# Causal masks of two attention kinds taken off TensorE, and whole-row running products, in a one-layer hybrid decoder on one Trainium2 core

## The chip, the core and the metric

The kernel runs on one core of a Trainium2 chip. A core has five engines that run their own queues of instructions in order and wait for each other by semaphores: TensorE (PE, with its weight loads shown apart as PEld), VectorE (DVE), ScalarE (ACT), GpSimd (POOL) and SyncE (SP, which here only issues DMAs). The metric is the device time of one execution in microseconds (us); lower is better. Work is in on-chip memory (SBUF, 128 partitions) and in the accumulators of TensorE (PSUM, eight banks).

## The reference

One decoder layer over one sequence of 2048 tokens of width 1024, in float32. The parts that matter here are the two causal attentions, eight heads of width 64 each:

```python
def forgetting_attention(q, k, v, log_f):            # FoX
    F = jnp.cumsum(log_f, axis=-1)
    ...
        s = jnp.einsum('bhqd,bhkd->bhqk', q_blk, k) * scale
        s = s + F_blk[..., None] - F[:, :, None, :]
        causal = kpos[None, :] <= qpos[:, None]
        s = jnp.where(causal, s, -jnp.inf)
        p = jax.nn.softmax(s, axis=-1)

def stick_breaking_attention(q, k, v):
    """A[t,s] = sigmoid(z_ts) * prod_{s<j<t} (1 - sigmoid(z_tj)), s < t"""
    ...
        strict = kpos[None, :] < qpos[:, None]
        log_one_minus_beta = jnp.where(strict, jax.nn.log_sigmoid(-z), 0.0)
        rest = lax.cumsum(log_one_minus_beta, axis=3, reverse=True) - log_one_minus_beta
        a = jnp.where(strict, jnp.exp(jax.nn.log_sigmoid(z) + rest), 0.0)

def reference(x, c, ...):
    h = rms_norm(x, g_attn) * (1.0 + scale_a) + shift_a          # scale, shift, gate from silu(c) @ w_ada
    q_f, k_f, v_f, q_s, k_s, v_s, f_logit = split(h @ w_in)
    log_f = jax.nn.log_sigmoid(f_logit + b_fgate)
    mix = concat(head_rms_norm(fox(...)), head_rms_norm(stick_breaking(...)))
    x = x + gate_a * (mix @ w_out)
    h = rms_norm(x, g_mlp) * (1.0 + scale_m) + shift_m
    u_gate, u_val = split(causal_depthwise_conv(h @ w_up))
    x = x + gate_m * ((silu(u_gate) * u_val) @ w_down)
    return rms_norm(x, g_final)
```

## The kernel before

The kernel works through three stages. First, attention in 32 units: a unit is a kind (`sb` for stick-breaking, then `fox`), a pair of heads `p` (0 to 3) and a block of 512 queries `tb` (0 to 3). While unit i attends, the projections of unit i+1 are interleaved (`interleave`); then follow the output projection, and the gated MLP (up, convolution, down). A scheduler places each instruction on its engine's queue by a simulation of the times, so the order on a queue isn't the order of the code, and projections may run some units ahead. What limits how far is the number of buffers that a tile's tag has: the buffers of a tag are used in turn in the order of the code, and a new tile waits until the last reader of the buffer is done.

Products in float32 precision are made from a high and a low part (`split`: ScalarE rounds the high part, another engine subtracts, lines 43 to 45).

Within a unit, each of two 256-query halves (`j`) and each of the two heads (`hl`) is a call of `sb_head` or `fox_head`. A half has two rows of 128 queries (`qi`). Row `qi` sees `(2 * j + qi + 1) * 128` keys, taken in chunks `ch` of 512 keys. `logits` (lines 382 to 388) makes one chunk in a bank of PSUM from two matmuls (there are two such banks); in the last chunk, which holds the diagonal, a third matmul in bf16 adds 1e30 to the masked places of the last 128 columns. The sign is turned, so that a large logit means no weight.

`sb_head` goes from the last chunk to the first. ScalarE makes `r` = sigmoid and `a` = sigmoid of the negated logits; VectorE turns `r` into a running product from right to left (line 426); `a` is multiplied by it (line 427), on VectorE where `(ch + qi) % 4 == 0` and on GpSimd otherwise. The product so far goes from one chunk's tile into the next as one copied column (line 424, GpSimd). `weighted` (lines 390 to 406) then transposes blocks of `a` on TensorE, splits them (ScalarE line 400, VectorE line 401) and multiplies them with V.

`fox_head` goes from the first chunk to the last. VectorE adds the forget sums `Fb` (a row of the cumulated sums on all partitions, a tile for each block of 512 keys and head) to the logits and keeps the running minimum (line 451), ScalarE takes the exponential of the whole row (line 455), and `weighted` follows.

`forget_sums` (lines 235 to 254) is called once, ahead of unit (sb,1,0). It loads the gate's logits, takes the logarithm of the sigmoid on ScalarE (Abs, Exp, Ln) and VectorE, stores it, loads it back with one head to a partition, and cumulates it in four scans of 512, each from the last column of the one before. Its tiles come from the tags `hf_a` and `z` of pool `px`, which else serve the projections of the first head pair.

`load_w` loads and splits the projection weights of a head pair; for `sb` the low parts are made by VectorE, for `fox` by GpSimd.

Pools lie on a stack: `px` and above it `sx` (tiles of the attention), which are both closed ahead of the first FoX unit, where `fx` is opened. A pool that is opened where others lay waits tile by tile for their last readers.

Of the kernel before, what the change touches and what calls it, by code (L numbers as in the profile page):

```python
# [16 lines left out]
P = 128  # L17
# [16 lines left out]
def kernel(ctx: ExitStack, tc: tile.TileContext, x, c, w_ada, b_ada, g_attn, w_in, b_fgate,  # L34
# [30 lines left out]
    ident = const.tile([P, P], F32, name="ident")  # L65
    make_identity(nc, ident)
    identb = const.tile([P, P], BF16, name="identb")
    make_identity(nc, identb)
    ones = const.tile([P, P], F32, name="ones")
    nc.vector.memset(ones, 1.0)  # L70
    masks = {}
    for kind, base in (("sb", -1), ("fox", 0)):
        m = masks[kind] = const.tile([P, P], BF16, name=f"mask_{kind}")
        nc.vector.memset(m, 0.0)
        nc.gpsimd.affine_select(out=m, in_=m, pattern=[[-1, P]], base=base, channel_multiplier=1,
                                compare_op=ALU.is_ge, fill=BIG)
# [8 lines left out]
    cols = const.tile([P, P + 40], F32, name="cols")  # L85
# [149 lines left out]
    def forget_sums():  # L235
        z = px.tile([NTB * NH, TB], F32, name="fz", tag="hf_a", bufs=2)
        e = px.tile([NTB * NH, TB], F32, name="fe", tag="z", bufs=2)
# [9 lines left out]
        for t in range(NTB):  # L247
            e = px.tile([NH, TB], F32, name="fl", tag="z", bufs=2)
            z = px.tile([NH, TB], F32, name="fc", tag="hf_a", bufs=2)
            nc.sync.dma_start(e, log_f[t * NH:(t + 1) * NH])  # L250
            nc.vector.tensor_tensor_scan(z, e, e, carry, ALU.add, ALU.bypass)
            carry = px.tile([NH, 1], F32, name="carry", bufs=2)
            nc.vector.tensor_copy(carry, z[:, TB - 1:TB])
            nc.sync.dma_start(fs[:, t * TB:(t + 1) * TB], z)

    def load_w(kind, p):
        base = (0 if kind == "fox" else 3 * 512) + p * P
        lo_engine = nc.vector if kind == "sb" else None
# [123 lines left out]
    def logits(kind, cw, need, qcols, hl, Q, K, last):  # L382
        b = qk()
        nc.tensor.matmul(b[:, :cw], Q[:, hl, 0, qcols], K[:, hl, :cw], start=True, stop=False)  # L384
        nc.tensor.matmul(b[:, :cw], Q[:, hl, 1, qcols], K[:, hl, :cw], start=False, stop=not last)  # L385
        if last:
            nc.tensor.matmul(b[:, need - P:need], identb, masks[kind], start=False, stop=True)
# [20 lines left out]
    def sb_head(j, qc, hl, Q, K, V, o):  # L408
        n = (2 * j + 2 + 3) // 4
        right = [None, None]  # L410
        for ch in range(n - 1, -1, -1):
            at = []
            for qi in range(2):
                need = min(512, (2 * j + qi + 1) * P - ch * 512)
                b = logits("sb", max(need, 2 * P), need, slice((qc + qi) * P, (qc + qi + 1) * P), hl, Q, K[ch],
                           ch == n - 1)
                r = sx.tile([P, 512 + 1], F32, name="r", bufs=7)
                a = sx.tile([P, 512], F32, name="a", bufs=7)
                nc.scalar.activation(r[:, :need], b[:, :need], AF.Sigmoid)  # L419
                nc.scalar.activation(a[:, :need], b[:, :need], AF.Sigmoid, scale=-1.0)  # L420
                if right[qi] is None:
                    nc.gpsimd.memset(r[:, need:need + 1], 1.0)
                else:
                    nc.gpsimd.tensor_copy(r[:, need:need + 1], right[qi][:, 0:1])
                rev = r[:, 0:need + 1][:, ::-1]
                nc.vector.tensor_tensor_scan(rev, rev, rev, 1.0, ALU.mult, ALU.bypass)  # L426
                (nc.vector if (ch + qi) % 4 == 0 else nc.gpsimd).tensor_mul(a[:, :need], a[:, :need], r[:, 1:need + 1])  # L427
# [4 lines left out]
            for m in range(0, nk, 2):  # L432
                kts = [4 * ch + m, 4 * ch + m + 1]
                weighted(o, kts, lambda kt, qi: at[qi][:, (kt - 4 * ch) * P:(kt - 4 * ch + 1) * P], V, hl,
                         ch == n - 1 and m == 0, ch == 0 and m == nk - 2, kts[0] == 2 * j)
                yield

    def fox_head(j, qc, hl, Q, K, V, o, Fb, ls):
        n = (2 * j + 2 + 3) // 4
        rows_ = []  # L440
        for qi in range(2):
            W = (2 * j + qi + 1) * P
            a = sx.tile([P, S], F32, name="p", bufs=4)
            mn = None
            for ch in range(n):
                need = min(512, W - ch * 512)
                b = logits("fox", max(need, 2 * P), need, slice((qc + qi) * P, (qc + qi + 1) * P), hl, Q, K[ch],
                           ch == n - 1)
                sl = slice(ch * 512, ch * 512 + need)
                m2 = sx.tile([P, 1], F32, name="mn", bufs=8)  # L450
# [211 lines left out]
    for i, u in enumerate(units):  # L662
        kind, p, tb = u
        nxt = units[i + 1] if i + 1 < len(units) else None
        if u == ("sb", 1, 0):
            forget_sums()
# [357 lines left out]
```

## Time and profile before

| what | us |
|---|---|
| median of 3 runs | 3146.88 |
| the three runs | 3148.08, 3141.64, 3146.88 |
| the profiled execution | 3145.07 |
| its span, first to last instruction | 3143.3 |
| TensorE, busy in the span | 2990.1 (95%) |
| VectorE | 2158.8 (69%) |
| ScalarE | 1652.0 (53%) |
| GpSimd | 1215.3 (39%) |

A row of a group names the line, the engine and the operation, what it writes and reads, the shapes and the count; then the busy time in us, the mean of one in ns, and the engine's idle time just before it with what ended it. A row of a timeline begins with the start in us and the length. A row of the waits gives the time in us, how often, and the longest. Busy time of TensorE includes the modelled ends of pipelined matmuls, so a busy TensorE can still be stalled for part of it. Of 3143.3 us, the stick-breaking units take up to 922 us, the FoX units those up to 1606 us, and the rest of the layer what is left.

### The profile page before, as it was taken

What the parts mean: (1) busy time and instruction counts of PE and PEld (TensorE: products, weight loads), DVE (VectorE), ACT (ScalarE), POOL (GpSimd) and SP (SyncE); (2) the same over time, 40 slices, a digit from 0 to 9 for tenths busy, and PEclk for the clock granted to TensorE, in tenths of its full rate; (3) what the DMA queues carried; (4) which work ended last, traced back from release to release, by engine and by line L of the source; (5) the groups of instructions that cost most, each with busy time, mean ns of one, the idle gap of its engine ahead of it and who ended that gap; (6) DMA issues with size and microseconds to landing.
All of it is one profiled execution on the core that took longest, in us unless ns stands there. A gap on an engine that the chain in (4) does not pass through costs nothing.

```text
span 3143.3 us, 46642 instructions
## 1 busy us (share of the span) xinstructions
PE 2990.1 (95%) x16190; PEld 2521.1 (80%) x16190; DVE 2158.8 (69%) x3343; ACT 1652.0 (53%) x3033; POOL 1215.3 (39%) x1391
## 2 busy tenths in 40 slices
PE   6899998999989999999999999999899998999998
PEld 5778787877878889888877678888678887888887
DVE  6787888978866775556843587777987776254253
ACT  5565666656756665556744444444444444343332
POOL 2563555647543132142112344444444442322321
PEclk8999999999999999999999999999999999999999
DMA  9447542455336695685546632222222223554552
GB/s 267 167 156 247 169 128 78 159 200 161 127 107 225 204 306 184 188 298 177 170 154 219 213 101 81 86 87 82 84 80 83 88 86 123 195 199 161 190 199 90
DMA packets 292941, 496.53 MB, mean 158 GB/s; under 512 B 29449, under 2 KB 177665, under 8 KB 291681
## 3 DMA queue, kind: packets, MB, share of 16 engines
q1 hardware_dynamic: 281072, 480.92, 47.9%
q10 hardware_dynamic: 11632, 12.63, 1.1%
q8 instruction: 128, 2.10, 0.3%
q14 instruction: 109, 0.88, 0.1%
HBM read 352.61 MB, written 90.51 MB: 141 GB/s over the span
## 4 chain that ended last, share of the span: by engine, by line
PE 57%; DVE 13%; DMA 12%; POOL 7%; issue 6%; ACT 4%; SPq 1%; ACTq 0%; POOLq 0%; DVEq 0%
PE ps_pj L287 8%; PE ps_o L963 8%; PE ps_pv L405 6%; PE ps_o L813 6%; PE ps_pt L396 5%; PE ps_pj L326 5%; PE ps_t L963 4%; PE ps_bc L963 4%; DMA wuraw<-in_w_up_dram 3%; PE ps_qk L384 3%; PE ps_qk L385 3%; DVE r L426 2%; DVE wu L45 2%; PE ps_t L813 2%; DMA Q<-q 2%
## 5 line engine op out<-in xcount | busy, mean ns | idle before, releaser
L813 PE MATMUL ps_o<-oa,wu 128*128 128x512 f32 x2088 | 503.3, 392 | 12.6 <-DVE oa L45 7.5
L813 PEld LDWEIGHTS ps_o<-oa,wu 128*128 128x128 f32 x2088 | 390.7, 188 | 104.2 <-DVE oa L45 11.8
L405 PE MATMUL ps_pv<-at,V 128*128 128x256 f32 x2304 | 416.4, 299 | 25.6 <-DVE at L401 12.5
L401 DVE TENSOR_TENSOR at<-ps_pt,at 128x512 fp32r<-128x512 f32 (+1 forms) x576 | 363.4, 651 | 109.1 <-ACT at L400 106.5
L400 ACT ACTIVATE at<-ps_pt 128x512 fp32r<-128x512 f32 (+1 forms) x576 | 315.7, 577 | 209.6 <-PE ps_pt L396 165.8
L287 PE MATMUL ps_pj<-hp,w_qk 128*128 128x512 f32 x1512 | 414.1, 405 | 11.9 <-POOL hp L45 3.4
L426 DVE TENSOR_TENSOR_SCAN r<-r 128x513 f32<-128x513 f32 (+2 forms) x320 | 383.6, 1213 | 40.2 <-ACT r L419 30.5
L427 POOL TENSOR_TENSOR a<-a,r 128x512 f32<-128x512 f32 (+3 forms) x240 | 280.3, 1171 | 310.5 <-DVE r L426 178.9
L405 PEld LDWEIGHTS ps_pv<-at,V 128*128 128x128 f32 x2304 | 339.0, 194 | 61.5 <-DVE at L401 25.1
L287 PEld LDWEIGHTS ps_pj<-hp,w_qk 128*128 128x128 f32 x1512 | 273.4, 190 | 65.8 <-POOL hp L45 4.5
L45 DVE TENSOR_TENSOR wd<-wdraw,wd 128x1024 fp32r<-128x1024 f32 x88 | 112.2, 1275 | 260.9 <-ACT wd L44 260.8
L384 PE MATMUL ps_qk<-K,Q 128*128 128x512 f32 (+2 forms) x640 | 269.5, 421 | 12.0 <-DMA K<-q 6.2
L45 POOL TENSOR_TENSOR g<-graw,g 128x512 fp32r<-128x512 f32 x84 | 141.4, 1685 | 325.9 <-ACT g L44 325.8
L963 PE MATMUL ps_o<-wd,g 128*128 128x512 f32 x1040 | 250.2, 390 | 8.8 <-ACT g L44 8.8
L326 PE MATMUL ps_pj<-w_v,hp 128*128 128x256 f32 (+1 forms) x1536 | 241.1, 293 | 3.8 <-DVE q L296 2.0
L813 PE MATMUL ps_t<-ob,wu 128*128 128x512 f32 x984 | 241.6, 390 | 0.0
L385 PE MATMUL ps_qk<-K,Q 128*128 128x512 f32 (+2 forms) x640 | 238.5, 373 | 0.0
L963 PEld LDWEIGHTS ps_o<-wd,g 128*128 128x128 f32 x1040 | 195.6, 188 | 49.8 <-ACT g L44 9.2
L44 ACT ACTIVATE wu<-wuraw 128x512 fp32r<-128x512 f32 x214 | 133.2, 626 | 184.4 <-PE ps_o L813 114.7
L326 PEld LDWEIGHTS ps_pj<-w_v,hp 128*128 128x128 f32 x1536 | 212.5, 194 | 13.3 <-DVE q L296 2.8
L813 PEld LDWEIGHTS ps_t<-ob,wu 128*128 128x128 f32 x984 | 184.8, 188 | 39.1 <-DVE wu L45 0.3
L396 PE MATMUL ps_pt<-ident,a 128*128 128x128 f32 x1088 | 185.6, 280 | 21.7 <-POOL a L427 13.2
(221 smaller groups left out, 5665.2 us busy)
## 6 DMA issues: line engine op xcount, KB each, us to landing
hp<-hs SPq DMA_DIRECT2D x224, 512.0 KB
wuraw<-in_w_up_dram SPq DMA_DIRECT2D x84, 512.0 KB
wdraw<-in_w_down_dram SPq DMA_DIRECT2D x84, 512.0 KB
Q<-q SPq DMA_DIRECT2D x128, 256.0 KB
g<-u SPq DMA_DIRECT2D x42, 512.0 KB
graw<-g SPq DMA_DIRECT2D x84, 256.0 KB
hs<-hp SPq DMA_DIRECT2D x32, 512.0 KB
K<-q SPq DMA_DIRECT2D x128, 128.0 KB
```

What stands on the lines that cost most here:

```text
L45: (lo_engine or nc.gpsimd).tensor_sub(lo, src, f(hi))
L287: nc.tensor.matmul(acc, w[kt][:, a, n], h[:, bb], start=kt == 0 and i == 0, stop=kt == KT - 1 and i == 2)
L326: nc.tensor.matmul(av[:, t * width:(t + 1) * width], hts[kt][:, a, tok], w[1][kt][:, bb, 0:width], start=kt == 0 and m == 0, stop=kt == KT ...
L384: nc.tensor.matmul(b[:, :cw], Q[:, hl, 0, qcols], K[:, hl, :cw], start=True, stop=False)
L385: nc.tensor.matmul(b[:, :cw], Q[:, hl, 1, qcols], K[:, hl, :cw], start=False, stop=not last)
L396: nc.tensor.transpose(b[:, i * P:(i + 1) * P], blk(kts[kk], qi), ident)
L400: nc.scalar.activation(at[:, 0, lo:], b[:, lo:], AF.Copy)
L401: nc.vector.tensor_sub(at[:, 1, lo:], b[:, lo:], f(at[:, 0, lo:]))
L405: nc.tensor.matmul(o[:, 0:2 * P], V[kt // 4][:, kt % 4, hl, :], rhs, start=first and kk == 0 and w == 0, stop=last and kk == 1 and w == 1)
L426: nc.vector.tensor_tensor_scan(rev, rev, rev, 1.0, ALU.mult, ALU.bypass)
L813: nc.tensor.matmul(b, w[:, p, j], o[:, q], start=first and i == 0, stop=last and i == 2, skip_group_check=True)
L963: nc.tensor.matmul(banks[t][n], g[:, a, t * P:(t + 1) * P], w[:, b, n * TB:(n + 1) * TB], start=k == 0 and i == 0, stop=k == NKD - 1 and i ...
```

## The change

Five things change together, all in the attention stage.

1. The bf16 mask matmul, its identity and its two mask tiles are gone. In `sb_head`, the first `r` of a row gets a 0 instead of a 1 in the column right of it, and its scan is `state = max(r * state, edge)`: `edge` is a tile of zeros with an identity in its last 128 columns but one, so that the running product is 0 right of the diagonal, 1 on it, and the product left of it. In `fox_head`, GpSimd makes for each row a copy `Fd` of the 128 forget sums under the diagonal with 1e30 in the masked places (`affine_select`), and the reduction of the last chunk is split in two: the columns left of the diagonal block with `Fb`, the block with `Fd`.
2. From unit (sb,0,3) on, pools `sx` and `px` are closed and a new `sx` is opened. There the `r` of a row is one tile of 2049 columns (`rw`, four buffers), so a chunk's scan starts from the column next to it, read as a scalar, and nothing is copied. `a` has eight buffers there. Units (sb,0,0) to (sb,0,2) keep chunk tiles and copies.
3. All products `a * r` are made by GpSimd.
4. The low parts of the weights of `sb` pairs 1 to 3 are made by GpSimd, too.
5. `forget_sums` takes its tiles from the tag `a` of the new `sx`, and `Fb` has eight buffers instead of nine.

```diff
-    ident = const.tile([P, P], F32, name="ident")
+    edge = const.tile([P, TB + 1], F32, name="edge")
+    nc.vector.memset(edge, 0.0)
+    ident = edge[:, TB - P:TB]
     make_identity(nc, ident)
-    identb = const.tile([P, P], BF16, name="identb")
...
     def forget_sums():
-        z = px.tile([NTB * NH, TB], F32, name="fz", tag="hf_a", bufs=2)
-        e = px.tile([NTB * NH, TB], F32, name="fe", tag="z", bufs=2)
+        z = sx.tile([NTB * NH, TB], F32, name="fz", tag="a", bufs=8)
+        e = sx.tile([NTB * NH, TB], F32, name="fe", tag="a", bufs=8)
...
-            e = px.tile([NH, TB], F32, name="fl", tag="z", bufs=2)
-            z = px.tile([NH, TB], F32, name="fc", tag="hf_a", bufs=2)
+            e = sx.tile([NH, TB], F32, name="fl", tag="a", bufs=8)
+            z = sx.tile([NH, TB], F32, name="fc", tag="a", bufs=8)
...
-        lo_engine = nc.vector if kind == "sb" else None
+        lo_engine = nc.vector if (kind, p) == ("sb", 0) else None
...
-        nc.tensor.matmul(b[:, :cw], Q[:, hl, 1, qcols], K[:, hl, :cw], start=False, stop=not last)
-        if last:
-            nc.tensor.matmul(b[:, need - P:need], identb, masks[kind], start=False, stop=True)
+        nc.tensor.matmul(b[:, :cw], Q[:, hl, 1, qcols], K[:, hl, :cw], start=False, stop=True)
...
+        whole = [sx.tile([P, S + 1], F32, name="rw", bufs=4) for _ in range(2)] if long_rows else None
...
-                if right[qi] is None:
-                    nc.gpsimd.memset(r[:, need:need + 1], 1.0)
+                if last:
+                    nc.gpsimd.memset(r[:, need:need + 1], 0.0)
+                elif not long_rows:
+                    nc.gpsimd.tensor_copy(r[:, need:need + 1], right[qi][:, 0:1])
+                if last:
+                    rev = r[:, 0:need + 1][:, ::-1]
+                    nc.vector.tensor_tensor_scan(rev, rev, edge[:, TB - need:TB + 1][:, ::-1], 0.0, ALU.mult, ALU.max)
+                elif long_rows:
+                    rev = r[:, 0:need][:, ::-1]
+                    nc.vector.tensor_tensor_scan(rev, rev, rev, r[:, need:need + 1], ALU.mult, ALU.bypass)
                 else:
-                    nc.gpsimd.tensor_copy(r[:, need:need + 1], right[qi][:, 0:1])
-                rev = r[:, 0:need + 1][:, ::-1]
-                nc.vector.tensor_tensor_scan(rev, rev, rev, 1.0, ALU.mult, ALU.bypass)
-                (nc.vector if (ch + qi) % 4 == 0 else nc.gpsimd).tensor_mul(a[:, :need], a[:, :need], r[:, 1:need + 1])
+                    rev = r[:, 0:need + 1][:, ::-1]
+                    nc.vector.tensor_tensor_scan(rev, rev, rev, 1.0, ALU.mult, ALU.bypass)
+                nc.gpsimd.tensor_mul(a[:, :need], a[:, :need], r[:, 1:need + 1])
...
+            diag = sx.tile([P, P], F32, name="Fd", bufs=3)
+            nc.gpsimd.affine_select(out=diag, in_=Fb[n - 1][:, (qc + qi) * P:(qc + qi + 1) * P], pattern=[[-1, P]],
+                                    base=0, channel_multiplier=1, compare_op=ALU.is_ge, fill=BIG)
...
+                parts = [(0, need, Fb[ch][:, :need])]
+                if ch == n - 1:
+                    parts = [(0, need - P, Fb[ch][:, :need - P])] * (need > P) + [(need - P, need, diag)]
+                for lo, hi, add in parts:
+                    m2 = sx.tile([P, 1], F32, name="mn", bufs=8)
+                    nc.vector.tensor_tensor_reduce(out=a[:, ch * 512 + lo:ch * 512 + hi], in0=b[:, lo:hi], in1=add,
+                                                   scale=1.0, scalar=3e38 if mn is None else mn, op0=ALU.add,
+                                                   op1=ALU.min, accum_out=m2)
+                    mn = m2
...
+        if u == ("sb", 0, NTB - 1):
+            tick(1 << 20)
+            close_pool("sx", "px")
+            sx = open_pool("sx", side="right")
+            long_rows = True
         if u == ("sb", 1, 0):
             forget_sums()
         if u == ("fox", 0, 0):
             tick(1 << 20)
-            close_pool("sx", "px")
+            close_pool("sx")
             sx = open_pool("fx", side="right")
         if kind == "fox" and tb == 0:
-            Fbs = [[sx.tile([P, TB], F32, name="Fb", bufs=9) for _ in range(NTB)] for _ in range(2)]
+            Fbs = [[sx.tile([P, TB], F32, name="Fb", bufs=8) for _ in range(NTB)] for _ in range(2)]
```

36 lines of the change are left out of this document (13 added, 23 removed).

## The prediction

> **What bounds the kernel now.** I read the page's totals first, then the windows by stage, the groups of instructions, and last the order of single instructions in a heavy stretch.
>
> ```profile
> span 3143.3 us, 46642 instructions
> PE 2990.1 (95%) x16190; PEld 2521.1 (80%) x16190; DVE 2158.8 (69%) x3343; ACT 1652.0 (53%) x3033; POOL 1215.3 (39%) x1391
> ...
> 72.00:922.00 850.00, 783.36 (x5008) 678.05 (x5008) 709.65 (x959) 547.40 (x1183) 468.58 (x692) 0.97 0.47 151
> 922.00:1606.00 684.00, 672.62 (x4479) 592.38 (x4477) 446.83 (x1150) 424.21 (x782) 173.54 (x217) 1.00 0.66 212
> 465.00:537.00 72.00, 60.75 (x366) 51.21 (x365) 65.53 (x83) 47.44 (x101) 43.46 (x63) 0.91 0.28 90
> 850.00:922.00 72.00, 61.42 (x367) 52.13 (x366) 60.51 (x74) 45.23 (x91) 41.44 (x54) 0.91 0.27 86
> 1000.00:1100.00 100.00, 99.49 (x642) 84.99 (x641) 73.34 (x183) 60.99 (x106) 14.45 (x20) 1.00 0.60 200
> 1472.00:1511.00 39.00, 36.85 (x261) 31.05 (x260) 34.10 (x99) 31.63 (x61) 4.43 (x11) 1.00 0.35 83
> ```
>
> A window's row gives the length, then the busy time of PE, PEld, DVE, ACT, POOL, then granted clock and DMA. The change touches two stages: stick-breaking attention (72 to 922 us) and FoX (922 to 1606). FoX is a TensorE stage: 672.6 of 684 us busy, 642 matmuls in 100 us. Stick-breaking is not: 783.4 of 850, and in two of its four heaviest units (last query block of a head pair, 465 to 537 and 850 to 922) 366 and 367 matmuls in 72 us, 5.1 per us, with DVE busy 65.5 and 60.5 us. There VectorE's queue sets the pace, and these are the rows that fill it:
>
> ```profile
> L426 DVE TENSOR_TENSOR_SCAN r<-r 128x513 f32<-128x513 f32 (+2 forms) x320 | 383.6, 1213 | 40.2 <-ACT r L419 30.5 <-POOL r L424 6.3 <-POOL r L422 1.0
> L427 POOL TENSOR_TENSOR a<-a,r 128x512 f32<-128x512 f32 (+3 forms) x240 | 280.3, 1171 | 310.5 <-DVE r L426 178.9 <-ACT a L420 42.4 <-ACT r L419 24.3
> L427 DVE TENSOR_TENSOR a<-a,r 128x512 f32<-128x512 f32 (+3 forms) x80 | 60.6, 757 | 6.0 <-ACT r L419 0.5
> L424 POOL COPY r<-r 128x1 f32<-128x1 f32 x192 | 105.5, 551 | 3.3 <-DVE r L426 3.0
> ```
>
> VectorE and GpSimd also stop each other. From the timelines of the two engines (start, length):
>
> ```profile
> 603.92 0.18 POOL L424 COPY r<-r 128x1 f32<-128x1 f32 x1
> 604.05 1.09 POOL L427 TENSOR_TENSOR a<-a,r 128x512 f32<-128x512 f32 x1
> 605.34 0.87 POOL L424 COPY r<-r 128x1 f32<-128x1 f32 x1
> 606.37 1.09 POOL L427 TENSOR_TENSOR a<-a,r 128x512 f32<-128x512 f32 x1 [0.17 <-DVE r L426]
> ...
> 604.63 1.59 DVE L426 TENSOR_TENSOR_SCAN r<-r 128x513 f32<-128x513 f32 x1
> 606.60 1.95 DVE L426 TENSOR_TENSOR_SCAN r<-r 128x513 f32<-128x513 f32 x1
> ```
>
> The scan that starts at 606.60 ends at 608.55, which is 1.09 us after the product of 606.37 ends (607.46); the one of 604.63 ends 1.08 us after the product's end at 605.14. A one-column copy, 0.18 us at 603.92, takes 0.87 us at 605.34 because it ends with the scan (606.21). So a scan and a GpSimd product take turns. [...]
>
> **The change part by part.** The sum is made against the profiled execution, 3145.07 us (span 3143.3); the median of three is 3146.88, 1.8 above it.
>
> *Masks off TensorE.*
>
> ```profile
> L387 PE MATMUL ps_qk<-mask_sb,identb 128*128 128x128 bf16 x128 | 30.5, 238 | 0.0
> ...
> 1006.86 0.23 PE L387 MATMUL ps_qk<-mask_fox,identb 128*128 128x128 bf16 x1
> 1006.90 1.40 PE L287 MATMUL ps_pj<-hp,w_qk 128*128 128x512 f32 x5
> ...
> 608.94 0.23 PE L387 MATMUL ps_qk<-mask_sb,identb 128*128 128x128 bf16 x1
> 609.01 0.61 PE L396 MATMUL ps_pt<-ident,a 128*128 128x128 f32 x4
> ```
>
> 256 matmuls go, 128 in each stage (the group of one is shown). Each lasts 0.23 us, but the next matmul starts 0.04 to 0.07 us after it, so its place in the queue is worth 0.045 us: 256 x 0.045 = 11.5 us, half in each stage. Bounds 10 (0.04) and 59 (0.23, no pipelining). [...]
>
> *VectorE's load in the stick-breaking stage.* All products go to GpSimd: 80 x 0.757 = 60.6 us leave VectorE. The weight splits of head pairs 1 to 3 also go there, 24 of w_qk and 8 of w_v:
>
> ```profile
> L45 DVE TENSOR_TENSOR w_qk<-raw_qk,w_qk 128x256 fp32r<-128x256 f32 x32 | 20.5, 654 | 3.1 <-ACT w_qk L44 3.1
> L45 DVE TENSOR_TENSOR w_v<-raw_v,w_v 128x256 fp32r<-128x256 f32 x16 | 8.1, 512 | 2.3 <-ACT w_v L44 2.1
> L45 POOL TENSOR_TENSOR w_qk<-raw_qk,w_qk 128x256 fp32r<-128x256 f32 x32 | 23.5, 750 | 28.3 <-ACT w_qk L44 28.3
> ...
> L426 DVE TENSOR_TENSOR_SCAN r<-r x320: 390/1220/2326, 72.5 to 906.9; 128x513 f32<-128x513 f32 x96, 128x129 f32<-128x129 f32 x32, 128x385 f32<-128x385 f32 x32
> L251 DVE TENSOR_TENSOR_SCAN fc<-fl,carry x3: 1261/1272/1273, 296.1 to 303.8; 8x512 f32<-8x512 f32 x3
> ```
>
> 24 x 0.654 + 8 x 0.512 = 19.8 us. Against it, 168 of the 192 copies go (24 stay in head pair 0 ahead of its last block), and their scans start from a pointer: 1.27 us in the row with a carry against the mean of 1.21, 168 x 0.06 = 10 us. The mult/max scan against the `edge` tile has no row; it has the same two inputs and length as the old one, so I take 0, between -5 and +5 us. More products of 1.09 us stand in the scans' way (the longest scan took 2.326 us, the median 1.220): scans fill 384 of 850 us, so of 80 more products 45% meet one, and hold it 0.5 us on average (0.5 and 0.86 in the two rows above, less the ones met at the end): an estimate of +18 us. Net: -60.6 - 19.8 + 10 + 18 = -52 us of 709.7.
>
> GpSimd pays 80 x 1.171 = 94 plus 25 for splits, and loses 168 x 0.551 = 93: +26 on 468.6 of 850, which it has room for. But taking turns, the two engines have as much to do as before: 80 x (1.09 - 0.757) = +27, +10 for the pointer, less 168 copies of about 0.18 (30). So VectorE's 52 us are worth between 0 (the turns bind) and 52 (its queue binds). I take half, 25 us: in the heavy units VectorE was busy 91% and 84%, but TensorE 84 and 85% too, and TensorE waits already for products that will now all come from the slower engine:
>
> ```profile
> PEld ps_pt L396 <- POOL a L427: 20.1, 21, 2.3
> ```
>
> *The forget sums.* They move from buffers of their own to the ring of eight `a` buffers, and take ten places of it between the last heads of unit (sb,0,3) and the first of (sb,1,0). In the order of the changed kernel as built, they stand right there on ACT and VectorE (the old order had them a unit earlier, among other work), and the last two loads of `fz` stand on SP's queue behind the store of `oT` of the finished unit. `a` of the next head comes after the first of their scans. The chain, from the old rows:
>
> ```profile
> 277.88 0.63 ACT L241 ACTIVATE fe<-fz 32x512 f32<-32x512 f32 x1 [2.15 <-DMA fz<-zs]
> 283.38 0.68 DVE L244 SCALAR_TENSOR_TENSOR fe<-fz,fe 32x512 f32<-32x512 f32 x1 [3.06 <-DMA hp<-hs]
> 284.09 0.32 SPq L245 DMA_DIRECT2D log_f<-fe  x1
> 285.94 0.73 SPq L250 DMA_DIRECT2D fl<-log_f  x2
> ...
> L419 ACT ACT_TABLE_LOAD x4 | 5.1, 1283 | 0.1
> ```
>
> About 2.5 for the loads, 3 x 0.63 + 2 x 1.28 for ACT, 0.68, 1.85 from store to load (284.09 to 285.94), 2 for that load (taken like the store), 1.27: 12.7 us without a new `a`, while logits wait for their two banks. TensorE has some 30 projection matmuls queued there (8 us, by the five in 1.40 us at 1006.90), and the next rows trickle behind the other three scans and stores, some 4 us: I take +9 (bounds +3 to +20). At the old place the forget sums left behind some -5 (0 to -8: two VectorE waits of 3 us and 2 on the loads).
>
> *New pool ahead of (sb,0,3)*: its first rows sit in memory that the old pools held; in the built order the first sigmoid waits for a GpSimd memset behind the last product of the unit before: +3 (0 to +8).
>
> *FoX.*
>
> ```profile
> masks.py:199 POOL TENSOR_SCALAR_AFFINE_SELECT ident<-ident x1: 292/292/292, 1.1 to 1.1; 128x128 f32<-128x128 f32 x1
> ...
> L451 DVE CUSTOM_DVE_ANT_0 p<-ps_qk,Fb,mn 128x512 f32<-128x512 f32 x120 | 89.3, 745 | 22.8 <-PE ps_qk L385 17.6 <-PE ps_qk L387 3.0
> L451 DVE CUSTOM_DVE_ANT_0 p<-ps_qk,Fb,mn 128x384 f32<-128x384 f32 x24 | 14.7, 611 | 3.7 <-PE ps_qk L387 3.6
> L451 DVE CUSTOM_DVE_ANT_0 p<-ps_qk,Fb,mn 128x128 f32<-128x128 f32 x24 | 8.2, 342 | 1.5 <-PE ps_qk L387 1.5
> L451 DVE DVE_READ_ACCUMULATOR2_ANT mn<- 128x1 f32 x320 | 26.4, 82 | 0.0
> ...
> POOL at L399 <- PE ps_pv L405: 177.2, 36, 19.7
> ```
>
> 128 selects of 0.292 (37 us) fall to GpSimd, 174 of 684 busy. 96 of 128 rows split their last reduction: 0.611 + 0.342 + 0.082 - 0.745 = 0.29 us, 28 us of VectorE. Most hides under TensorE; in the light units (1472 to 1511: VectorE 34.1 of 39, and the like block of pair 1) it does not: 18 splits, +5 (0 to 28). New waits: VectorE's diagonal reduction waits for its select, which stands on GpSimd behind memsets that wait for TensorE (177.2 us in 36 waits; behind VectorE then queue `at` and the row's exponential). Three `Fd` buffers keep the select about three rows ahead, so I take +3 with the ninth `Fb` buffer gone (the loads of the next pair wait on SP until the old pair's last head is done): 0 to +15.
>
> Sum: -11.5 - 25 + 9 - 5 + 3 + 5 + 3 = -21.5. 3145.1 - 21.5 = 3123.6, and 1.8 for the median: **3125 us**.
>
> **The rivals.** *VectorE's queue was all that held the heavy units.* For it: 5.1 matmuls per us there against 6.4 in FoX. Then the 52 us count in full, and the other terms stay: -21.5 - 27 = -48.5, and 3098. Against it: two engines that take turns.
>
> *The turns bind* (slower). The engines' common work does not fall (+27 + 10 - 30), products come at 1.09 instead of 0.757 us, and the 20.1 us that TensorE's loads wait for products grow by half. Place: units of block 3. Then -11.5 + 0 + 10 + the forget sums' +20 - 5 + 3 + 8 = +24.5: 3171. It decides where scans and products together fill over nine tenths of a heavy unit. The rows show the turns, but not that they fill a unit. [...]
>
> *GpSimd's queue in FoX* gives the gain back: selects late behind memsets, +15 instead of +3 and VectorE's splits at +15 instead of +5: about 3147, no change.
>
> That whole rows serialize a head (a sigmoid waiting for products of the same tile) I leave out: in the built order, within a row, it waits for TensorE alone.
>
> **How the numbers follow.** Forecast 0.42, queue in full 0.18, no change 0.15, turns 0.25. The runs before spread over 6.4 us, so 0.2% (6.3 us) is what can be told. Faster: 0.41 + 0.18 + 0.04 = 0.63; same 0.12; slower 0.25. Range 3085 to 3165: the full gain is inside, half of the turns' case is outside. The forecast's own range is 3105 to 3140.
>
> **What would show it.** In the changed profile: TensorE with 256 fewer matmuls; stick-breaking stage some 25 to 30 us shorter, VectorE near 660 busy, heavy units near 68 us; a hole of about 10 us on TensorE and VectorE where the forget sums run; FoX within 8 us of 684. Wrong if heavy units stay at 72 with scans' mean over 1.35 us (turns), if TensorE's waits for products pass 40 us, or if FoX grows by over 15.

## The result: 0.5% slower

The changed kernel took 3160.62 us (median of four runs, 3156.77 to 3161.92) against 3144.26 for the kernel before in the same sitting: a ratio of 1.005 [1.0033, 1.0068], some 16 us slower. The forecast was 3125. The ratios further down are each against the kernel before, on the same chip; 0.001 is 3.15 us, and an interval is about 4 us to either side, so a difference of two ratios is good to some 6 us.

The profiled execution took 3160.99 us. Its page's totals, then the windows that answer to those of before (length, busy PE, PEld, DVE, ACT, POOL, granted clock, DMA share, GB/s): the two stages, then the last unit of head pair 1 and of head pair 3.

```profile
span 3159.2 us, 46407 instructions
PE 2964.1 (94%) x15934; PEld 2510.7 (79%) x15934; DVE 2129.2 (67%) x3422; ACT 1650.8 (52%) x3033; POOL 1316.8 (42%) x1459
...
72.00:922.00 850.00, 760.65 (x4876) 666.51 (x4875) 657.90 (x846) 546.11 (x1181) 530.34 (x636) 0.97 0.48 151
922.00:1622.00 700.00, 668.65 (x4354) 591.00 (x4352) 465.25 (x1342) 423.73 (x783) 210.40 (x346) 0.99 0.65 208
479.60:548.70 69.10, 56.12 (x377) 47.96 (x376) 62.83 (x73) 49.17 (x104) 49.07 (x53) 1.00 0.31 96
855.40:922.90 67.50, 54.68 (x357) 46.31 (x356) 57.25 (x66) 45.09 (x91) 43.26 (x40) 1.00 0.29 91
```

The stick-breaking stage ends where it ended (922.9 us, before 922.2), although VectorE does 52 us less in it and its heavy units fell from 72 us to 69.1 and 67.5. FoX takes 698.9 us instead of 683.8: TensorE has less to do (668.65, before 672.62) and stands 31 us idle instead of 11. The rest of the span is as before.

From the end of one unit's last output to that of the next, the time went up in (sb,0,2), from 74.1 to 79.5 us, and in (sb,1,0), from 19.3 to 44.4; it fell in (sb,0,3), from 98.9 to 93.9, and in (sb,1,1), from 42.3 to 34.2. Work moves between units, so no single unit's time is the price of a part. Two holes stand out. The first is at the start of unit (sb,0,3), where the new pool opens. Timelines of VectorE, GpSimd, ScalarE and TensorE there:

```profile
253.72 0.42 DVE L519 TENSOR_TENSOR oT<-ps_pv,o 64x256 f32<-64x256 f32 x1 [1.85 <-ACT o L518]
267.35 1.00 DVE L424 TENSOR_TENSOR_SCAN rw<-rw,edge 128x129 f32<-128x129 f32 x2
...
257.91 0.13 POOL L418 MEMSET rw<- 128x1 f32 x2 [3.05 <-PE ps_pt L497]
265.43 0.60 ACT L289 ACTIVATE q<-ps_pj 128x512 fp32r<-128x512 f32 x1 [8.64 <-PE ps_pj L281]
266.61 0.27 ACT L415 ACTIVATE rw<-ps_qk 128x128 f32<-128x128 f32 x1
257.65 8.42 PE L281 MATMUL ps_pj<-hp,w_qk 128*128 128x512 f32 x36
```

From the last output of the unit before (253.72) to the first scan of the new one (267.35) it is 13.6 us. In between ScalarE waits 8.64 us for projections, with the first sigmoid of a new row behind that wait, and TensorE runs 36 projection matmuls in one go. Before, it was 1.5 us from the one to the other:

```profile
248.86 0.42 DVE L510 TENSOR_TENSOR oT<-ps_pv,o 64x256 f32<-64x256 f32 x1 [1.39 <-ACT o L509]
250.37 0.43 DVE L426 TENSOR_TENSOR_SCAN r<-r 128x129 f32<-128x129 f32 x1 [0.28 <-ACT r L419]
```

The second is the forget sums at (sb,1,0):

```profile
347.60 0.42 DVE L519 TENSOR_TENSOR oT<-ps_pv,o 64x256 f32<-64x256 f32 x1 [1.12 <-ACT o L518]
355.14 0.68 DVE L238 SCALAR_TENSOR_TENSOR fe<-fz,fe 32x512 f32<-32x512 f32 x1 [7.13 <-ACT fe L237]
354.48 0.63 ACT L237 ACTIVATE fe<-fe 32x512 f32<-32x512 f32 x1
355.14 0.60 ACT L44 ACTIVATE q<-ps_pj 128x512 fp32r<-128x512 f32 x1
355.77 0.69 DVE L45 TENSOR_TENSOR q<-ps_pj,q 128x512 fp32r<-128x512 f32 x1
356.51 9.04 PE L281 MATMUL ps_pj<-hp,w_qk 128*128 128x512 f32 x30 [9.36 <-DVE q L45]
365.83 0.55 ACT L416 ACTIVATE a<-ps_qk 128x128 f32<-128x128 f32 x2
...
348.00:357.00 9.00, 0.49 (x1) 0.49 (x2) 1.33 (x3) 5.05 (x6) 0.61 (x1) 0.50 0.68 183
357.00:366.00 9.00, 8.55 (x30) 6.49 (x29) 5.73 (x8) 4.02 (x8) 5.21 (x5) 0.80 0.50 115
```

TensorE's 30 projection matmuls do not fill this hole as the prediction had it: they wait for the split of an earlier `q`. Its high part stands on ScalarE's queue right behind the logarithm of the forget sums (`fe`, which ends at 355.11), its low part on VectorE's behind `fe`. So TensorE stands 9.36 us, the granted clock is 0.50 in the first of the two windows at the end and 0.80 in the second, where its projections run, and the next `a` is made 17.8 us after the last output has ended.

### The profile page after: what moved, and what is told of

Its sections match the earlier page's. It is cut to its first block, busy times and chain, and to the rows that moved or that the text cites. A ratio compares the mean times of both kernels' runs of the same rounds, so it can differ in the third digit from the quotient of the medians.

```text
span 3159.2 us, 46407 instructions
## 1 busy us (share of the span) xinstructions
PE 2964.1 (94%) x15934; PEld 2510.7 (79%) x15934; DVE 2129.2 (67%) x3422; ACT 1650.8 (52%) x3033; POOL 1316.8 (42%) x1459
## 5 line engine op out<-in xcount | busy, mean ns | idle before, releaser
L828 PE MATMUL ps_o<-oa,wu 128*128 128x512 f32 x2088 | 503.1, 392 | 13.2 <-DVE oa L45 8.2
L397 PE MATMUL ps_pv<-at,V 128*128 128x256 f32 x2304 | 415.5, 297 | 26.4 <-ACT at L392 11.9
L431 POOL TENSOR_TENSOR a<-a,rw 128x512 f32<-128x512 f32 (+2 forms) x272 | 332.3, 1237 | 208.3 <-DVE rw L427 82.8
L281 PEld LDWEIGHTS ps_pj<-hp,w_qk 128*128 128x128 f32 x1512 | 280.7, 194 | 87.3 <-DMA hp<-hs 12.4
L378 PE MATMUL ps_qk<-K,Q 128*128 128x512 f32 (+2 forms) x640 | 260.8, 409 | 15.3 <-ACT a L416 5.0
L427 DVE TENSOR_TENSOR_SCAN rw<-rw 128x512 f32<-128x512 f32 x168 | 242.1, 1460 | 19.0 <-ACT rw L415 18.5
L379 PE MATMUL ps_qk<-K,Q 128*128 128x512 f32 (+2 forms) x640 | 235.1, 369 | 0.0
L388 PE MATMUL ps_pt<-edge,a 128*128 128x128 f32 x1088 | 186.2, 279 | 42.9 <-POOL a L431 40.1
```

The lines of the kernel that those rows point to most:

```text
L281: nc.tensor.matmul(acc, w[kt][:, a, n], h[:, bb], start=kt == 0 and i == 0, stop=kt == KT - 1 and i == 2)
L397: nc.tensor.matmul(o[:, 0:2 * P], V[kt // 4][:, kt % 4, hl, :], rhs, start=first and kk == 0 and w == 0, stop=last and kk == 1 and w == 1)
L427: nc.vector.tensor_tensor_scan(rev, rev, rev, r[:, need:need + 1], ALU.mult, ALU.bypass)
L431: nc.gpsimd.tensor_mul(a[:, :need], a[:, :need], r[:, 1:need + 1])
L828: nc.tensor.matmul(b, w[:, p, j], o[:, q], start=first and i == 0, stop=last and i == 2, skip_group_check=True)
```

## The experiments

A scheduler orders every build anew, so an edit can also shift work that it does not touch. All runs were timed in five rounds.

### FoX or the forget sums?

Run 1 gives the forget sums buffers of their own in the changed kernel:

```diff
-        z = sx.tile([NTB * NH, TB], F32, name="fz", tag="a", bufs=8)
+        z = sx.tile([NTB * NH, TB], F32, name="fz", tag="fz", bufs=1)     # fe, fl, fc likewise
```

> The changed kernel, with the forget sums in two buffers of their own (tags fz and fe, one buffer each) instead of the ring of a. Theory A (the hole at (sb,1,0) is made by the ring): the unit falls from 44 us to 19 to 22, the unit after it gives back the 8 us that it had gained, the whole falls by 13 to 19 us against the changed kernel, to about 3144. Rival (the hole is the price of whole rows and of all products on GpSimd at the start of a head pair): less than 4 us.

Measured: 3163.68 us, 1.0038 [1.0026, 1.0050]. By the medians the ring of `a` costs some 4 us, which is inside the noise of this difference and is not the loss. The traces say more: (sb,1,0) falls from 44.4 to 17.7 us, (sb,0,3) rises from 93.9 to 109.0, and the stick-breaking stage as a whole falls from 850.9 to 840.2. But FoX, whose code is the same, takes 709.4 us instead of 698.9.

Run 2 keeps the changed stick-breaking and takes back FoX's mask matmul, unsplit reduction and no select (eight `Fb` buffers stay).

> The changed kernel, with FoX as before: a bf16 mask matmul in the last chunk, one reduction per chunk, no select; eight Fb buffers. Theory B (select and split reduction cost more than 128 mask matmuls): the FoX stage falls from 700 us to 682 to 690, the whole by 10 to 18 us, to about 3146. Rival (the FoX stage is longer for its ninth Fb buffer, or for what the stage before leaves): under 4 us.

Measured: 3145.69 us, 0.9981 [0.9971, 0.9991].

Run 3 puts FoX's part alone into the kernel before.

> The kernel before, with the FoX part of the change alone: select, split reduction, eight Fb buffers. Stick-breaking as before. Theory B: 8 to 18 us slower than before, about 3156, all of it between 922 and 1622 us. Rival (the FoX part is free by itself): within 4 us of before.

Measured: 3163.39 us, 1.0040 [1.0024, 1.0056]: FoX's part by itself costs 13 us.

Run 4 joins runs 1 and 2.

> Both at once: the changed stick-breaking stage with the forget sums in buffers of their own, FoX as before. If A and B hold and add: 25 to 35 us under the changed kernel, 3126 to 3136, so 10 to 18 us faster than before, which is what the relief of VectorE was forecast to bring. If relief brings nothing: 3142 to 3148.

Measured: 3140.74 us, 0.9967 [0.9955, 0.9979]: 10 us faster than the kernel before.

### What in FoX

Run 5 is the kernel before with FoX's mask matmul left out and nothing in its place, run 6 splits its last reduction as well, run 7 is run 3 with six `Fd` buffers. The main line of run 6's edit:

```diff
+                parts = [(0, need - P, Fb[ch][:, :need - P])] * (need > P) + [(need - P, need, Fb[ch][:, need - P:need])]
```

> The kernel before with FoX's causal mask left out altogether: the 128 mask matmuls of the FoX stage go, and nothing takes their place (no select, no split reduction; the causal mask is missing from FoX, so only the time is read). Term of the prediction: 128 x 0.045 = 6 us faster (0.998 of the kernel before), FoX stage about 678 instead of 684. Rival 1: the next matmul starts 0.04 to 0.07 us after the mask anyway, and VectorE's turn in the light units sets the end: 0 to -2 us. Rival 2: the price is the whole duration of 0.23 us, 29 us.

Measured: 3145.01 us, 0.9970 [0.9959, 0.9982].

> As the kernel with FoX's mask left out, but each row's last reduction is split in two, at the diagonal block, both parts with the plain Fb tile: no select on GpSimd, no Fd tile, nine Fb buffers (the causal mask is missing from FoX). Theory 'the split costs': VectorE's 96 more reductions of 0.29 us lie on the path of a row: 10 to 17 us slower than the kernel without mask, so +5 to +11 against the kernel before. Theory 'GpSimd's selects cost': within 3 us of the kernel without mask, about 5 us faster than before, since the select and its three buffers are what costs the +11 of the FoX part alone.

Measured: 3151.80 us, 1.0005 [0.9996, 1.0014].

> The kernel before with the FoX part of the change alone (+0.4% in its run), but six Fd buffers instead of three. GpSimd waited 185.6 us in 80 waits for VectorE's reduction to free an Fd buffer, and its memsets of the transposed tiles stand behind that. Theory 'GpSimd is held by Fd': with six buffers the +11 falls to 5 or less. Theory 'the split costs': no change, +10 to +12.

Measured: 3162.73 us, 1.0038 [1.0026, 1.0051]. TensorE, VectorE and SyncE have the same order of instructions as in run 3, and ScalarE's differs in a few places; GpSimd's is another.

Run 8 is run 6 with eight `Fb` buffers (run 6 has nine) and with selects that nothing reads.

> As the kernel with FoX's mask left out and the last reduction split (stage of 685.6 us, ratio 1.0005), with eight Fb buffers, and GpSimd makes the 128 selects into three Fd buffers, but no instruction reads them (the causal mask is missing from FoX): GpSimd never waits for VectorE to free an Fd buffer, VectorE never waits for a select. Theory 'GpSimd is held': GpSimd's waits for VectorE put its other work (products for the late weights, memsets of the transposed tiles) late; without them no more than 3 us on top of the split kernel. Theory 'the selects' own work and their readings of Fb cost': +10 or more, as in the FoX part alone (698.7 us, 1.004).

Measured: 3152.32 us, 1.0008 [0.9999, 1.0017]: selects and the ninth buffer together cost nothing that could be timed.

So the mask matmuls are worth 9.5 us in FoX, the split costs 11 back, the selects 1, and that the reduction reads the select another 10 (run 3 against run 8, +- 6). The FoX windows of before and of runs 5, 6 and 3, in this order:

```profile
922.20:1606.00 683.80, 672.42 (x4478) 592.22 (x4476) 446.63 (x1149) 424.21 (x782) 173.54 (x217) 1.00 0.66 212
```
```profile
925.20:1602.80 677.60, 659.33 (x4352) 588.13 (x4350) 446.55 (x1150) 423.05 (x782) 173.13 (x217) 1.00 0.67 214
```
```profile
927.50:1613.10 685.60, 664.17 (x4352) 590.42 (x4350) 463.84 (x1342) 422.67 (x782) 172.67 (x217) 1.00 0.65 212
```
```profile
922.80:1621.50 698.70, 671.36 (x4352) 595.05 (x4350) 463.70 (x1342) 423.36 (x782) 209.10 (x345) 0.98 0.65 208
```

Without the masks TensorE is busy 13.1 us less: 0.10 us for each of 128, not 0.045. In run 5's trace 6.2 of these 13 us come out of the stage, and by the medians 9.5. From run 6 to run 3 the same 4352 matmuls keep TensorE busy 7 us longer: the granted clock fell from 1.00 to 0.98. Where it falls is seen at run 3's hole of 3.40 us:

```profile
1268.00:1270.00 2.00, 0.03 (x1) 0.00 (x0) 0.00 (x0) 1.45 (x3) 0.68 (x1) 1.00 1.10 182
1270.00:1276.50 6.50, 4.93 (x21) 4.63 (x22) 3.66 (x7) 3.58 (x9) 1.81 (x2) 0.50 0.97 215
1276.50:1280.00 3.50, 3.50 (x22) 3.15 (x21) 0.00 (x0) 1.01 (x2) 0.21 (x1) 0.95 0.43 171
```

TensorE stops at 1268.03 and starts again at 1271.43; the clock is halved from 1270.0 for some 6.8 us (the 0.95 of the last row is the rest of it). By windows of 1 us through the FoX stage, such stretches come once in the kernel before (3.4 us of full-speed work lost, summed as 1 minus the clock), once in run 6 (3.4), twice in run 8 (5.1), four times in run 3 (11.9), three times in the changed kernel (5.1). In these traces the length of a hole alone does not tell what follows. In the kernel before, a hole of 2.46 us (at 1258.31), with another of 1.29 us 0.9 us behind it, was followed by half clock from 1262.3, while one of 2.46 us in run 6 (at 943.88) left it at 1.00. The windows of before:

```profile
1258.00:1260.80 2.80, 0.34 (x4) 0.16 (x3) 0.05 (x1) 2.80 (x5) 2.49 (x2) 1.00 1.05 360
1262.30:1269.10 6.80, 6.02 (x26) 5.72 (x27) 3.93 (x7) 3.54 (x8) 0.00 (x0) 0.50 1.01 213
```

A hole of the changed kernel that the one before has not, in the rows of SyncE and TensorE, and SyncE's rows of before:

```profile
1053.55 7.99 SPq L690 DMA_DIRECT2D Fb<-fs  x4
1061.59 0.90 SPq L346 DMA_DIRECT2D hp<-hs  x2
...
1067.59 2.93 PE L281 MATMUL ps_pj<-hp,w_qk 128*128 128x512 f32 x6 [2.94 <-DMA hp<-hs]
```
```profile
1051.98 6.43 SPq L675 DMA_DIRECT2D Fb<-fs  x4
1058.46 0.90 SPq L352 DMA_DIRECT2D hp<-hs  x2
```

The loads of the next pair's `Fb` hold SyncE's queue until the old pair's last head has read its tiles. With the split (7.85 us in run 6) that takes 1.5 us longer, the loads of `hs` stand behind it, and the projections run dry. This is one hole of the changed kernel and not the account of the split: in run 6, where the split alone is timed, TensorE waits less for `hs` than in run 5:

```profile
PE ps_pj L287 <- DMA hp<-hs: 4.6, 4, 2.4
```
```profile
PE ps_pj L287 <- DMA hp<-hs: 1.9, 2, 1.5
```

What makes the split cost 11 us stays open.

### What in stick-breaking

Runs 9 and 10 vary run 4: one product in four back on VectorE everywhere, or only ahead of (sb,0,3).

```diff
-                nc.gpsimd.tensor_mul(a[:, :need], a[:, :need], r[:, 1:need + 1])
+                (nc.vector if (ch + qi) % 4 == 0 else nc.gpsimd).tensor_mul(...)       # run 10: and not long_rows
```

> The fastest kernel so far (changed stick-breaking, forget sums in buffers of their own, FoX as before; 10 us faster than the kernel before), with one product in four back on VectorE as in the kernel before: chunks and rows with (ch + qi) divisible by 4. It asks whether the move of the products to GpSimd gave anything. Prediction (VectorE's queue binds in half): 80 x 0.757 = 60 us back on VectorE, 15 to 25 us slower, so about +10 against the kernel before. Rival 'the turns bind': scan and GpSimd product take turns, so the move gave nothing: 0 to 10 us faster than without this edit, -10 to -20 against the kernel before; units (sb,0,2) and (sb,0,3) get 5 and 10 us back.

Measured: 3159.70 us, 1.0026 [1.0016, 1.0036]: 19 us slower than run 4.

> The fastest kernel so far (changed stick-breaking, forget sums in buffers of their own, FoX as before; ratio 0.9967), with one product in four back on VectorE only in head pair 0 ahead of its last query block, where the one-column copies remain on GpSimd: with all products there GpSimd was busy 116 of 182 us and unit (sb,0,2) was 5 us longer than before. Theory 'GpSimd's queue holds that unit': it gets its 5 us back, 3 to 7 us faster than without this edit, about 0.995 of the kernel before. Theory 'the move pays everywhere' (as it did in the run with products shared throughout, 18 us): 0 to 4 us slower than without it.

Measured: 3130.53 us, 0.9936 [0.9923, 0.9949], the lowest ratio of all: 10 us faster than run 4, 28 faster than run 9. Moving the products to GpSimd pays 28 us where rows are whole and costs 10 where the copies still stand on GpSimd's queue: unit (sb,0,2), where 4 of these 10 us are seen, takes 79.0 us in run 4 and 75.1 in run 10.

Run 11 is the kernel before with the stick-breaking mask alone moved into the scan (and eight `Fb` buffers).

> The kernel before with stick-breaking's 128 mask matmuls taken out and the mask made by the mult/max scan against the edge tile; products, copies, splits and forget sums as before. Prediction: 128 x 0.045 = 6 us faster and the scan at no cost, ratio 0.998. In FoX the masks were worth 0.10 us each of TensorE's busy time and half of it came out as time. Theory 'TensorE is not what ends a unit here': 0 to 3 us faster, since VectorE's queue sets the pace. If the mult/max scan is dearer than the mult scan: slower by 128 times the difference, at most 10.

Measured: 3136.68 us, 0.9954 [0.9941, 0.9966]. The 14 us from the masks and the 19 of the products are more than the whole part of run 4 gives: some 20 us go elsewhere. The 14 us are a net figure, too. The windows of the stick-breaking stage and of the rest of the layer, before and in run 11:

```profile
72.00:922.20 850.20, 783.56 (x5009) 678.21 (x5009) 709.84 (x959) 547.40 (x1183) 468.58 (x692) 0.97 0.47 151
1606.00:3143.30 1537.30, 1486.46 (x6509) 1211.81 (x6509) 956.52 (x1118) 637.61 (x974) 557.38 (x451) 0.99 0.41 132
```
```profile
72.00:900.10 828.10, 762.14 (x4871) 667.66 (x4871) 700.37 (x956) 543.08 (x1179) 455.87 (x692) 0.98 0.48 155
1581.90:3131.00 1549.10, 1506.48 (x6509) 1215.86 (x6509) 971.74 (x1117) 639.98 (x974) 575.79 (x451) 0.99 0.40 131
```

The stage is 22 us shorter. The rest of the layer, where nothing was edited, is 12 us longer, with VectorE and GpSimd busy 15 and 18 us more. Runs 16 and 17 below, built on run 11, have that longer rest too (1551.3 and 1551.1 us), run 4 has 1544.6, and all others 1537 to 1543; why is open. So a price that is read from run 11 against the kernel before, or from run 17 against run 4, holds time of a stage that the edit does not touch.

Runs 12 to 15 start from run 10. Run 12 calls the forget sums at (sb,2,0), run 13 puts the weight splits back on VectorE, run 14 scans without a pointer, run 15 swaps the pools at (sb,1,0).

> As the kernel with products shared in head pair 0 ahead of its last block, with the forget sums asked for at unit (sb,2,0) instead of (sb,1,0). In the fastest kernel so far the stretch from the end of (sb,0,2) to the end of (sb,1,0) is 126.8 us against 118.2 in the kernel before, and both the forget sums and the new pool stand in it. Theory 'the forget sums cost there': they move among the work of head pair 1, 3 to 8 us faster than without this edit. Theory 'the new pool costs': no change, within 2 us.

Measured: 3134.16 us, 0.9949 [0.9934, 0.9964].

> The fastest kernel so far (products of head pair 0 ahead of its last block shared with VectorE, all others on GpSimd; ratio 0.9936), with the weight splits of head pairs 1 to 3 back on VectorE as in the kernel before. Prediction: 19.8 us go back on VectorE, of which half counts: 10 us slower. Theory 'GpSimd is the queue that binds from (sb,0,3) on' (108.9 of 169.4 us busy there against 76.4 of 160.5 before, and TensorE waits 21 us for products): splits off GpSimd's queue bring products earlier, 3 to 8 us faster.

Measured: 3129.78 us, 0.9949 [0.9936, 0.9961].

> As the fastest kernel so far, but the scans of a row's chunks to the left of its last one start from 1.0 and take in the column they continue from (513 columns in place of 512 with a pointer), as the kernel before does, without the copies since the row is whole. Pointer scans last 1.448 us on average, scans of 513 columns in the kernel before 1.401. Prediction: 168 x 0.06 = 10 us less on VectorE, half of it counts: 5 us faster. [...]

Measured: 3135.16 us, 0.9961 [0.9947, 0.9974].

> As the fastest kernel so far, but the new pool and the whole rows begin at unit (sb,1,0), not at (sb,0,3); (sb,0,3) runs with rows by chunk, copies and shared products. Theory 'the heavy unit (sb,0,3) with the next pair's projections is where GpSimd binds': the stretch of 169.4 us from (sb,0,3) to (sb,1,1) falls towards the 150.1 of the kernel with the stick-breaking masks alone changed, 8 to 15 us faster. Theory 'the swap of pools or the forget sums cost': no gain, within 3 us, the hole only moves.

Measured: 3131.93 us, 0.9953 [0.9941, 0.9966]. None of the four gains, and without pointers (run 14) the kernel is 8 us (+- 6) slower than run 10, where the prediction had pointers cost 5. In run 15 the long unit moves with the swap: (sb,0,3) falls from 114.9 to 96.4 us, (sb,1,0) rises from 22.1 to 30.7. So run 16 adds the swap alone to run 11 (with the `tick` that first empties the list of the old unit's deferred work), and run 17 the closing of `px` and the forget sums in buffers of their own:

```diff
+        if u == ("sb", 0, NTB - 1):
+            tick(1 << 20)
+            close_pool("sx")                # run 17: close_pool("sx", "px")
+            sx = open_pool("sx", side="right")
```

> The kernel with the stick-breaking masks alone changed (ratio 0.9954, 14 us faster than the kernel before), and ahead of unit (sb,0,3) the pool of the attention rows is closed and opened again at its old place and size: nothing else moves, the new tiles only wait for the old ones. Prediction's price for the new pool: +3 (0 to +8). Theory 'the swap holds the unit up': +8 to +15, the stretch from (sb,0,3) to (sb,1,1) goes from 150 us to some 160. Theory 'the swap is free, the rest of the new form costs': within 3 us of 0.9954.

Measured: 3148.29 us, 1.0002 [0.9993, 1.0011]: the swap costs 15 us. In its trace the stick-breaking stage is 8.4 us longer than in run 11 (836.5 us, from 828.1).

> As the run with the swap alone, but the pool of the projections is closed with it as in the change, and the forget sums take buffers of their own in the new pool. Prediction: +3 for the pool, forget sums now beside other work, +4 at most: ratio about 0.997. If the forget sums or the closing of the projections' pool are what costs: 0.999 to 1.003 where the swap alone is near 0.9955.

Measured: 3154.77 us, 1.0021 [1.0011, 1.0031]: another 6 (the stage takes 845.5 us, 9.0 more). The stretch from (sb,0,3) to the end of (sb,1,1) in runs 11, 16 and 17:

```profile
248.10:398.20 150.10, 141.66 (x857) 121.49 (x856) 131.40 (x184) 100.34 (x221) 72.13 (x120) 1.00 0.67 216
```
```profile
248.90:406.70 157.80, 145.70 (x856) 124.39 (x856) 131.09 (x184) 103.25 (x224) 75.69 (x123) 0.97 0.64 205
```
```profile
247.70:417.60 169.90, 152.53 (x886) 129.75 (x886) 135.46 (x188) 103.66 (x226) 83.57 (x124) 0.96 0.61 202
```

Runs 11 and 16 do the same 856 or 857 matmuls. With the swap the stretch is 7.7 us longer: TensorE's idle time goes from 8.4 to 12.1 us, and it is busy 4.0 us longer with the clock at 0.97 instead of 1.00. The pause at the swap itself is short here, on VectorE 3.7 us from the start of the last output to that of the first scan (1.8 in run 11):

```profile
248.47 0.42 DVE L515 TENSOR_TENSOR oT<-ps_pv,o 64x256 f32<-64x256 f32 x1 [1.75 <-ACT o L514]
252.17 1.11 DVE L429 TENSOR_TENSOR_SCAN r<-r,edge 128x129 f32<-128x129 f32 x2
```

Emptying the deferred work and the swap of the pool were not run apart.

Last, run 18 masks FoX in run 10 by one select over the whole last chunk, so that no reduction is split.

> As the fastest kernel so far, with FoX's mask matmuls out: GpSimd selects the whole last chunk of a row from Fb into one Fd buffer of 512 columns, and the last reduction stays in one piece. Theory 'the split costs' : masks -9 and no split, so up to 9 us faster if the select's wait costs nothing. Theory 'a reduction that waits for a select costs': +1 to +10 slower, since with one buffer GpSimd starts a select only when the row before has been reduced.

Measured: 3142.91 us, 0.9985 [0.9976, 0.9994]: 15 us slower than run 10, although 128 masks (9.5 us in run 5) are gone and nothing is split. FoX takes 693.1 us, 681.2 in run 10, and VectorE waits 12.2 us for selects. Whether more buffers would help was not run.

## Why the prediction was wrong

The measured prices, beside the terms of the sum: by the medians of two neighbouring runs, and by what the stage in question lost or gained in their traces. In the traces stages of the same code differ, too: the old stick-breaking took 847 to 856 us in the kernel before and the five runs that leave it unchanged, the changed FoX 698.7 to 709.4 in three.

| step | predicted | by medians, us | its stage in the traces, us |
|---|---|---|---|
| masks off TensorE, stick-breaking | -5.8 | -14.5 (run 11) | -22 |
| masks off TensorE, FoX | -5.8 | -9.5 (run 5) | -6 |
| VectorE's relief: products, splits, pointers | -25 | -17 (run 17 to run 4) | -6.5 |
| new pool ahead of (sb,0,3) | +3 | +15 (run 11 to run 16) | +8 |
| forget sums moved (+9 - 5) | +4 | +10 (run 16 to 17, with the closing of `px`: 6; ring of `a`, run 4 to 2: 4) | +18 (9 and 9) |
| FoX: split reductions | +5 | +11 (run 5 to run 6) | +8 |
| FoX: selects and their waits | +3 | +11 (run 6 to run 3) | +13 |

**The failed steps** are one gain that the prediction put too high and costs that it kept small. VectorE's relief was to give 25 us and gave 17, of which 6.5 in its own stage. "New pool ahead of (sb,0,3)", put at +3 with a bound of 8, cost 15; the forget sums, put at +4, cost 10, and 18 in their stage; the two terms of FoX, put at +8 together, cost 22. The masks gave more than forecast, and not enough to make up for it.

The new pool was read as the wait of one memset. In the changed kernel this memset does wait (3.05 us), but 13.6 us pass there without a scan, while ScalarE and TensorE run projections; in run 16's stretch the loss is half idle time of TensorE and half matmuls at a lower clock. That the lost overlap of two units makes the price is argued from these rows, not shown. FoX's split was sized by the light units alone; what makes it 11 us stays open. And **no term carried the clock**: the hole of 3.40 us in run 3 cost another 3.4 us in half-speed matmuls.

**Masks off TensorE**: the sign was right, the size half of what it is. The spacing from a mask matmul to the next instruction (0.04 to 0.07) is not what the queue gains; in FoX 0.10 is. In stick-breaking TensorE is busy 21 us less in run 11; by an estimate 13 of them are masks at that price, and the rest goes with the granted clock (0.97 before, 0.98 in run 11).

**VectorE's load** was right: 657.9 us busy against "near 660", heavy units at 69.1 and 67.5 against "near 68". But those times were met in part by luck, for run 11, which leaves VectorE's load as it was, has 70.0 and 69.7 there:

```profile
455.50:525.50 70.00, 59.76 (x364) 52.05 (x363) 64.36 (x83) 48.78 (x105) 43.19 (x64) 0.90 0.28 91
830.40:900.10 69.70, 58.44 (x356) 50.05 (x355) 58.20 (x73) 43.60 (x89) 40.89 (x54) 0.93 0.27 88
```

And what fell from before to the changed kernel is TensorE's busy time, with the clock at 1.00 instead of 0.91; its idle time in the two units rose, from 11.3 to 13.0 us and from 10.6 to 12.8. That it is worth half, -25, came out at -17 for all of it, and -28 for the products of whole rows alone. The weight splits count for nothing that run 13 can tell, and the pointer scans gained (run 14); the mult/max scan costs what the plain one does (mean over 128x513: 1.365 us in the whole rows of the changed kernel, 1.401 for the plain scan before).

**The forget sums** made the hole that was described: 9.36 us of TensorE against an estimate of 9. From the end of the last output to the next `a` it took 17.8 us, not 12.7, and the projections that should have covered part of it were caught behind `fe` on ScalarE and VectorE.

**The turns bind**, the slower rival, gave 3171 and is nearest in time, but it is not what happened: with products back on VectorE the kernel is 19 us slower (run 9), so taking turns did not eat the relief. That a scan and a GpSimd product take turns shows in the changed kernel, too (the scan of 512 columns at 434.82 us lasts 1.95 us and ends 1.08 us after the product beside it, where the median of such scans is 1.28 us), but it did not decide. The rival's sign "scans' mean over 1.35" did not show: over all 320 scans of `r` the mean is 1.28 us, 1.21 before. The sign "waits for products pass 40" did:

```profile
PEld ps_pt L388 <- POOL a L431: 56.3, 52, 2.0
PE ps_pt L388 <- POOL a L431: 40.1, 46, 1.5
```

Before, these were 20.1 and 13.2 us. They nearly tripled, and the move still paid, so the sign was badly set.

**GpSimd's queue in FoX** had the sizes (+15 and +15; measured +11 and +11) but not the mechanism. GpSimd waits for VectorE to free `Fd`, 183.8 us with three buffers (run 3) and 152.7 with six (run 7), and the time does not change:

```profile
POOL Fd L445 <- DVE mn L457: 183.8, 83, 9.5
```
```profile
POOL Fd L445 <- DVE mn L457: 152.7, 70, 9.1
```

VectorE waited for a select once in run 3 (4.2 us). That the +10 for reading it comes from the order that the scheduler then makes, and the holes and half clock in it, is only argued: no run changed the order alone.

**What stays open.** The medians of the table add up to about +6 and its stages to about +12, the kernel is at +16. FoX's part costs 13 us beside the stick-breaking of before and 22 beside the changed one (run 4 to run 1, and run 2 to the changed kernel). In the traces its stage grows by 14.9 us beside the old one (run 3) and by 17.4 and 25.7 beside the new; why was not settled. That the range of 3085 to 3165 held the time is luck: it was drawn around a gain, and the time went the other way.

## What to carry to other kernels

Price the seams of a change, not only its instructions: a pool that was swapped between two units cost 15 us here, about what its contents gained. An operation that saves TensorE's time is worth that only if nothing else comes later for it: FoX's masks gave 9.5 us, and what replaced them took 22. And compare stages as well as whole times: a stage that an edit does not touch moved by 12 us. The best version here kept the mask matmuls in FoX and moved work to GpSimd only where GpSimd's queue had been cleared first.

## What the runs showed of the hardware

A halt of TensorE of 3.40 us was followed by some 6.8 us at half clock (run 3, above). Its length alone did not decide: of two halts of 2.46 us, one, with another of 1.29 us 0.9 us behind it, was followed by 6.8 us at half clock (kernel before, at 1258.31) and one left the clock at 1.00 (run 6, at 943.88). The hole of run 3 so cost another 3.4 us of full-speed work, and with the same 4352 matmuls TensorE was busy 7 us longer in run 3 (671.36 us) than in run 6 (664.17). A bf16 mask matmul of 128 columns between float32 matmuls took 0.10 us of TensorE's time (13.1 us for 128, run 5 against the kernel before), while the next matmul started 0.04 to 0.07 us after it. GpSimd's selects of 128x128 cost nothing that could be timed while nothing read them (128 of them with one `Fb` buffer less, 1 us with an interval of 4, run 8 against run 6).
